# A hybrid decoder layer on one core: moving operands stored as two runs, even and odd columns, and another table of loading rates

## The chip, the core and the metric

The kernel runs on one core of a Trainium2 chip. The core has a matrix engine (TensorE: PE in the profile for its products, PEld for the loads of its stationary operand), a vector engine (VectorE, DVE), a scalar engine (ScalarE, ACT), GpSimd (POOL) and a sync engine (SyncE, SP), which here issues the transfers. Sixteen DMA engines move data between main memory and the on-chip memory; products are summed in an accumulation memory of eight banks. The metric is the device time of one launch in microseconds (us), the median of several runs; lower is better.

## The reference

One decoder layer over 256 tokens of width 2048, in float32. A condition vector `c` yields nine modulation vectors, three for each of three blocks:

```python
cond = jax.nn.silu(c)
mod = cond @ ada_w[l] + ada_b[l]
sh1, sc1, gt1, sh2, sc2, gt2, sh3, sc3, gt3 = jnp.split(mod, N_MOD, axis=-1)
h = ada_in(x, norm_g[l, 0], sh1, sc1)              # rmsnorm(x) * g * (1 + sc) + sh
x = x + MACARON_W * gt1[:, None, :] * swiglu(h, ffn_w_gate[l, 0], ffn_w_up[l, 0], ffn_w_down[l, 0])
h = ada_in(x, norm_g[l, 1], sh2, sc2)
x = x + gt2[:, None, :] * hybrid_mixer(h, ...)     # 8 heads of attention with forgetting, 8 of a gated delta rule
h = ada_in(x, norm_g[l, 2], sh3, sc3)
x = x + MACARON_W * gt3[:, None, :] * swiglu(h, ffn_w_gate[l, 1], ffn_w_up[l, 1], ffn_w_down[l, 1])
return rmsnorm(x, final_norm)
```

`swiglu(h)` is `(silu(h @ wg) * (h @ wu)) @ wd` with an inner width of 5632. The three matrices of each SwiGLU, the mixer's input projection and its output projection are nearly all of the arithmetic; `ada_w` (2048 by 18432) is a matrix that meets a single vector.

## The kernel before, in words

**Layout.** Activations stand with features on the 128 partitions and tokens in the columns: `x` is 16 feature blocks (`k`) of 256 tokens. A weight matrix is cut into tiles of 128 by 128, 5392 in all. The host packs them in the order of use, eight to a block, so that 674 blocks of 512 KB are read one after the other.

**Products in two parts.** Each operand is split into a high part, which is its rounding to `fp32r`, the form in which TensorE takes a float32 operand in one pass, and a low part, which is what the rounding left. A product is high x high + high x low + low x high. `hs` holds the modulated input, per `k` 256 columns of the low part (`LO`) and then 256 of the high part (`HI`), with 64 columns of room behind them; `hid` holds the inner activations of a SwiGLU and `oh` the outputs of the heads, as [high | low], 256 columns each. The weight tile is the stationary operand and the activation is the moving one, column by column as it lies in memory, except in `project_rows` (the mixer's z and v parts), where a slice of 128 tokens of `hs` is stationary and 512 columns of weights move.

The shapes of the products are three. `gate_up_first` (the gate and up products of the first part of SwiGLU_1, lines 518 to 520) and `project` (the mixer's input projection, lines 706 to 708) give a weight tile three products of 256 columns. `mm_h` (the other gate and up products, lines 432 and 433) and `mm` (the down products and the output projection, lines 436 and 437) give it one of 512 columns, both parts of the activation side by side, and one of 256. `Early.products` (the first group of SwiGLU_2, lines 376 to 378) has three products, two of them of 258 columns, since two columns with the shift vector ride along.

**The stream of weights.** `Stream.block` issues the transfer of a block (`wraw`, line 96) and has ACT make its high part (`whi`, line 98); `Stream.next` has DVE make its low part (`wlo`, line 110) when the first tile of the block is used. There are four sets of buffers during a SwiGLU and three in the mixer.

**Modulation columns.** `ada_col` loads 128 rows of `ada_w` (1024 KB, into `adat`, line 228) and lets DVE multiply and sum them against `silu(c)` in one instruction (line 230), which gives one column of `mod`. There are 144 such columns. When each is loaded is set by `RATE`: a pair (b, r) says that from weight block b on, r columns are begun per block. `ada_need` brings forward those that a consumer asks for. Weight blocks 0 to 111 are the gate and up products of the first part of SwiGLU_1 (28 of its 44 inner blocks), 112 to 167 the down products of that part, 168 to 263 its second part, 264 on the mixer. Since each load is issued behind the last weight transfer (`issue_after(W.last)`), both kinds share one queue, SP's, in this order.

**Who writes the moving operands.** `modulate_one` (lines 317 to 328) and `Early.y` (lines 351 to 361) write `hs`: ACT the high part, DVE the low part. `split` (lines 449 to 451) writes `hid`, and `out_split` (lines 1070 to 1074) writes `oh`, with one instruction of ACT and one of DVE each.

## Time and profile before

| | us |
|---|---|
| median of 3 runs | 2041.44 |
| lowest and highest | 2040.09, 2043.89 |
| profiled execution, span from first to last instruction | 2038.5 |
| PE busy in it | 1998.6 (98%) |
| PEld busy | 1818.5 (89%) |
| DVE busy | 1566.0 (77%) |
| ACT busy | 1021.5 (50%) |
| POOL busy | 64.7 (3%) |

The profile gives no time of its own for the profiled execution beside its span. The transfers moved 519.56 MB, 255 GB/s on average. A line of the groups reads: line, engine, operation, out<-in, shape, count, then busy time and the mean of one in ns, then the idle time of the engine just before. A matrix product's own duration is longer than the distance to the next one, since products overlap in the array; what a product costs is the distance between starts, which the timeline shows. A window's row gives the busy time of each engine in a stretch of the span with the number of its instructions, then the granted clock as a share of full speed, the share of the DMA engines and what they moved in GB/s.

### The profile page before, as it was taken

To read this page: it belongs to the slowest core of one execution; us is meant where nothing else is said; L and a number is where in the kernel's file an instruction comes from. 1 tells how busy PE (TensorE), PEld (TensorE's weight loads), DVE (VectorE), ACT (ScalarE), POOL (GpSimd) and SP (SyncE) were. 2 spreads that over 40 slices of the span, in tenths; PEclk is the share of its full clock that TensorE was granted. 3 is DMA by queue.
4 is the path that set the end of the run, shared out by engine and by line. 5 is a ranking of instruction groups with operands and counts; after the bars stand their busy time and mean duration, and the time that the engine had idled before them with its cause. 6 is when DMAs were issued, how large, how long until landed. Compare 5 with 4: busy or idle time off the path is not lost.

```text
span 2038.5 us, 33631 instructions
## 1 busy us (share of the span) xinstructions
PE 1998.6 (98%) x13058; PEld 1818.5 (89%) x13059; DVE 1566.0 (77%) x2424; ACT 1021.5 (50%) x1607; POOL 64.7 (3%) x60
## 2 busy tenths in 40 slices
PE   8999999999999999999999999999999999999997
PEld 6999999888888888889989988988888888888886
DVE  6898978889888998779878889976666555555555
ACT  6544544333444446666655655654444344444442
POOL 0000000000000120000000002000000000000012
PEclk9999999999999999999999999999999999999998
DMA  9999867999889885676666668667776655555553
GB/s 338 350 327 327 288 212 262 372 344 368 334 338 331 336 306 187 232 243 236 219 242 221 222 229 304 234 223 241 252 231 218 193 188 189 193 187 191 192 187 113
DMA packets 129489, 519.56 MB, mean 255 GB/s; under 512 B 18217, under 2 KB 21545, under 8 KB 111153
## 3 DMA queue, kind: packets, MB, share of 16 engines
q1 hardware_dynamic: 129330, 517.42, 72.1%
q8 instruction: 102, 1.67, 0.3%
q14 instruction: 57, 0.47, 0.1%
HBM read 512.89 MB, written 4.47 MB: 254 GB/s over the span
## 4 chain that ended last, share of the span: by engine, by line
PE 86%; DVE 6%; ACT 2%; DMA 2%; issue 2%; SPq 0%; DVEq 0%; ACTq 0%
PE pd L436 15%; PE pu L432 10%; PE pg L432 10%; PE pd L437 8%; PE pu L433 5%; PE pg L433 5%; PE pgu L520 5%; PE pgu L518 5%; PE pgu L519 5%; PE pp L706 3%; PE pp L708 3%; PE pp L707 3%; DVE wlo L110 2%; DMA wraw<-in_w_dram 2%; PE po L436 2%
## 5 line engine op out<-in xcount | busy, mean ns | idle before, releaser
L110 DVE TENSOR_TENSOR wlo<-wraw,whi 128x1024 fp32r<-128x1024 f32 x674 | 822.5, 1228 | 307.2 <-ACT whi L98 304.3
L98 ACT CAST whi<-wraw 128x1024 fp32r<-128x1024 f32 x674 | 702.0, 1049 | 630.2 <-issue 153.4
L436 PE MATMUL pd<-hid,whi 128*128 128x512 f32 x1408 | 488.5, 390 | 0.0
L437 PE MATMUL pd<-hid,wlo 128*128 128x256 f32 x1408 | 397.3, 282 | 1.0 <-DVE wlo L110 0.8
L230 DVE CUSTOM_DVE_ANT_0 adat<-adat,cs,colt 128x2048 f32<-128x2048 f32 x140 | 329.3, 2352 | 35.9 <-DMA adat<-in_ada_dram 35.7
L432 PE MATMUL pg<-hs,whi 128*128 128x512 f32 x912 | 318.9, 390 | 0.5 <-DVE shc L384 0.4
L432 PE MATMUL pu<-hs,whi 128*128 128x512 f32 x912 | 318.7, 390 | 0.0
L436 PEld LDWEIGHTS pd<-hid,whi 128*128 128x128 f32 x1408 | 264.1, 188 | 55.0
L437 PEld LDWEIGHTS pd<-hid,wlo 128*128 128x128 f32 x1408 | 266.1, 189 | 3.0 <-DVE wlo L110 2.7
L433 PE MATMUL pg<-hs,wlo 128*128 128x256 f32 x912 | 257.2, 282 | 0.0
L433 PE MATMUL pu<-hs,wlo 128*128 128x256 f32 x912 | 257.1, 282 | 0.0
L518 PE MATMUL pgu<-hs,whi 128*128 128x256 f32 x896 | 249.0, 281 | 6.8 <-ACT hs L323 5.7
L520 PE MATMUL pgu<-hs,wlo 128*128 128x256 f32 x896 | 248.0, 281 | 1.9 <-DVE wlo L110 1.8
L519 PE MATMUL pgu<-hs,whi 128*128 128x256 f32 x896 | 249.8, 281 | 0.0
L432 PEld LDWEIGHTS pg<-hs,whi 128*128 128x128 f32 x912 | 171.1, 188 | 36.7 <-ACT shc L383 0.5
L432 PEld LDWEIGHTS pu<-hs,whi 128*128 128x128 f32 x912 | 171.1, 188 | 35.7
L706 PE MATMUL pp<-hs,whi 128*128 128x256 f32 x656 | 189.7, 290 | 2.4 <-ACT whi L98 1.2
L708 PE MATMUL pp<-hs,wlo 128*128 128x256 f32 x656 | 186.2, 285 | 0.3 <-DVE wlo L110 0.3
L707 PE MATMUL pp<-hs,whi 128*128 128x256 f32 x656 | 185.7, 283 | 0.0
L518 PEld LDWEIGHTS pgu<-hs,whi 128*128 128x128 f32 x896 | 168.7, 189 | 7.7 <-ACT hs L323 6.1
L433 PEld LDWEIGHTS pu<-hs,wlo 128*128 128x128 f32 x912 | 172.3, 189 | 0.2
L433 PEld LDWEIGHTS pg<-hs,wlo 128*128 128x128 f32 x912 | 172.4, 189 | 0.0
(334 smaller groups left out, 2572.0 us busy)
## 6 DMA issues: line engine op xcount, KB each, us to landing
wraw<-in_w_dram SPq DMA_DIRECT2D x674, 512.0 KB, 4.4
adat<-in_ada_dram SPq DMA_DIRECT2D x140, 1024.0 KB, 7.1
xr<-in_xr_dram SPq DMA_DIRECT2D x4, 512.0 KB, 6.3
adaf<-in_ada_dram SPq DMA_DIRECT2D x4, 512.0 KB, 8.7
adaf<-in_ada_dram SPq DMA_DIRECT2D x2, 1024.0 KB, 12.5
xd<-x SPq DMA_DIRECT2D x4, 512.0 KB, 8.3
rw<-rowd SPq DMA_DIRECT2D x16, 128.0 KB, 6.7
x<-xd SPq DMA_DIRECT2D x4, 512.0 KB, 8.8
```

Source lines behind the costliest of these rows:

```text
L98: self.cast = self.nc.scalar.copy(self.h, r).ins
L110: nc.vector.tensor_tensor(self.l, r, self.h.bitcast(F32), ALU.subtract)
L230: V.tensor_tensor_reduce(t, t, cs, 1.0, L("adab", q, 1), ALU.mult, ALU.add, mod[:, q : q + 1])
L432: PE.matmul(ps, wt[0], hs[:, k, ALL], start=(k == 0), stop=False)
L433: PE.matmul(ps[:, T:], wt[1], hs[:, k, HI], start=False, stop=(k == KD - 1))
L436: PE.matmul(ps, wt[0], act.rearrange("p a t -> p (a t)"), start=first, stop=False)
L437: PE.matmul(ps[:, :T], wt[1], act[:, 0], start=False, stop=last)
L518: PE.matmul(o, wh, hs[:, k, HI], start=first and s == 0, stop=False, skip_group_check=skip)
L519: PE.matmul(o, wh, hs[:, k, LO], start=False, stop=False, skip_group_check=skip)
L520: PE.matmul(o, wl, hs[:, k, HI], start=False, stop=last, skip_group_check=skip)
L706: PE.matmul(pp[i][:, :T], wh, hs[:, k, HI], start=(k == 0), stop=False)
L708: PE.matmul(pp[i][:, :T], wl, hs[:, k, HI], start=False, stop=(k == KD - 1))
```

## The change

**The layout.** `hs` now holds, per `k`, four runs of 144 columns: low part even tokens, low part odd tokens, high part even, high part odd; 128 are used (129 in the high part, for the two shift columns). The room per `k` is 576 columns as before. A product reads the two runs of a part in turn, one column from the even run, one from the odd, so that it gets the tokens in the same order as before and its output lies as before. `hid` and `oh` keep their 256 columns a part and hold even tokens in the first 128 and odd ones in the last 128. The writers (`modulate_one`, `Early.y`, `split`, `out_split`) read their sources in order and write into the two runs in turn (`pairs` for the source, `woven` or `part` for the destination). In the mixer's input `hs` stays as it was (`plain`, `weave=False`), since `project_rows` uses it as the stationary operand; there the weights move, and the host packs each 512 of their columns as 256 even ones and 256 odd ones, which are read in turn as well. The three products of `project` read and multiply as before.

No instruction is added or taken away by this, and no size of one changes.

**The rates.** From block 68 to 111 the columns are loaded at 0.2 a block instead of 0.06, from 112 to 167 at 0.38 instead of 0.5, from 168 to 263 at 0.34 instead of 0.38, from 280 to 407 at 0.27 instead of 0.25.

On SP's queue, from the weight blocks of the sixties on (`wraw` are weight blocks, `adat` modulation columns, `cstt` a table of constants of the mixer), before:

```order
L228 DMA adat<-in_ada_dram 128x2048
L96 DMA wraw<-in_w_dram 128x1024 x6
L664 DMA cstt<-in_cst_dram 128x1180
L96 DMA wraw<-in_w_dram 128x1024 x6
L228 DMA adat<-in_ada_dram 128x2048
L96 DMA wraw<-in_w_dram 128x1024 x17
L228 DMA adat<-in_ada_dram 128x2048
L96 DMA wraw<-in_w_dram 128x1024 x16
L228 DMA adat<-in_ada_dram 128x2048
L96 DMA wraw<-in_w_dram 128x1024 x2
```

and after:

```order
L240 DMA adat<-in_ada_dram 128x2048
L107 DMA wraw<-in_w_dram 128x1024 x4
L240 DMA adat<-in_ada_dram 128x2048
L107 DMA wraw<-in_w_dram 128x1024 x4
L683 DMA cstt<-in_cst_dram 128x1180
L107 DMA wraw<-in_w_dram 128x1024
L240 DMA adat<-in_ada_dram 128x2048
L107 DMA wraw<-in_w_dram 128x1024 x5
L240 DMA adat<-in_ada_dram 128x2048
L107 DMA wraw<-in_w_dram 128x1024 x5
```

Where two columns stood between runs of 16 and 17 weight blocks, there is now one for every five; behind block 112, where one stood for every two blocks, there is one for every two or three.

On DVE, at the last sums of the gate and up products of the first part (`tg` and `tu` are the gate and up sums of an inner block, `hid` its activation, `wlo` a weight block's low part, the ISA row with `adat` a modulation column), before:

```order
L536 TENSOR_TENSOR tg_2878<-pgu_2817,acc_425 128x256
L537 TENSOR_TENSOR tu_2879<-pgu_2817,acc_425 128x256
L110 TENSOR_TENSOR wlo_2992<-wraw_2988,whi_2990 128x1024
L467 TENSOR_TENSOR tu_2879<-tu_2879,tg_2878 128x256
L451 TENSOR_TENSOR hid_2884<-tu_2879,hid_2884 128x256
L110 TENSOR_TENSOR wlo_3032<-wraw_3028,whi_3030 128x1024
L230 ISA adat_3064,mod_126<-adat_3064,cs_86,colt_87 128x2048
```

and after:

```order
L121 TENSOR_TENSOR wlo_2965<-wraw_2961,whi_2963 128x1024
L555 TENSOR_TENSOR tg_2881<-pgu_2820,acc_425 128x256
L556 TENSOR_TENSOR tu_2882<-pgu_2820,acc_425 128x256
L242 ISA adat_2967,mod_126<-adat_2967,cs_86,colt_87 128x2048
L242 ISA mod_126 128x1
L486 TENSOR_TENSOR tu_2882<-tu_2882,tg_2881 128x256
L121 TENSOR_TENSOR wlo_2998<-wraw_2994,whi_2996 128x1024
L470 TENSOR_TENSOR hid_2887<-tu_2882,hid_2887 128x128x2
```

A column's product has come in between the sums and the low parts of the weights, and `hid` is written as 128 pairs. On PE the order of the products of the two SwiGLUs stays; in the mixer the heads' small products stand some projection tiles earlier or later in places.

The diff:

```diff
@@ -31,7 +31,7 @@
 GR = 24
 NEG = -1e30
 
-RATE = ((0, 0.5), (24, 0.34), (56, 0.45), (68, 0.06), (112, 0.5), (168, 0.38), (264, 0.1), (280, 0.25), (408, 0.125))
+RATE = ((0, 0.5), (24, 0.34), (56, 0.45), (68, 0.2), (112, 0.38), (168, 0.34), (264, 0.1), (280, 0.27), (408, 0.125))
 N_BIG, N_GDN = 3, 3
 N_FIRST = 4
 AHEAD = 4
@@ -40,7 +40,8 @@
 HIDX = 3
 MORE = True
 
-HS = 2 * 256 + 64
+HA = 128 + 16
+HS = 4 * HA
 PAD = {"hs": 16, "w": 56, "hid": 16, "more": 56}
 
 BACK = (4, 6, 9)
@@ -70,6 +71,16 @@
 N_COL = _n
 
 
+def woven(ap):
+
+    return ap.rearrange("p (a b) -> p b a", a=2)
+
+
+def pairs(ap):
+
+    return ap.rearrange("p (b a) -> p b a", a=2)
+
+
 class Stream:
 
 
@@ -113,9 +124,10 @@
                 self.owed -= 1.0
                 self.side()
         for d in range(width):
-            self.order.append((mat, k, n + d))
+            self.order.append((mat, k, n, width, d))
         o = (i % WB) * P
-        return self.h[:, o : o + width * P], self.l[:, o : o + width * P]
+        h, l = self.h[:, o : o + width * P], self.l[:, o : o + width * P]
+        return (h, l) if width == 1 else (woven(h), woven(l))
 
 
 @with_exitstack
@@ -311,21 +323,27 @@
 
 
     hsf = keep.tile([P, KD * HS + PAD["w"]], F32R, name="hs")
-    hs = hsf[:, : KD * HS].rearrange("p (k i) -> p k i", k=KD)
-    LO, HI, HIS, ALL = slice(0, T), slice(T, 2 * T), slice(T, 2 * T + 2), slice(0, 2 * T)
-
-    def modulate_one(j, g1, sh, r):
+    hs = hsf[:, : KD * HS].rearrange("p (k q a b) -> p k q a b", k=KD, q=2, a=2)
+    LO, HI = 0, 1
+
+    plain = hsf[:, : KD * HS].rearrange("p (k i) -> p k i", k=KD)[:, :, : 2 * T].rearrange("p k (q t) -> p k q t", q=2)
+
+    def part(k, q, extra=0):
+        return hs[:, k, q, :, : P + extra].rearrange("p a b -> p b a")
+
+    def modulate_one(j, g1, sh, r, weave=True):
 
         t = pt("ht")
+        hl, hh, tt = (part(j, LO), part(j, HI), pairs(t)) if weave else (plain[:, j, LO], plain[:, j, HI], t)
         V.scalar_tensor_tensor(t, x[:, j], g1, r, ALU.mult, ALU.mult)
         if j % 2:
             A.activation(t, t, AF.Identity, bias=sh)
-            A.copy(hs[:, j, HI], t)
-            return V.tensor_tensor(hs[:, j, LO], t, hs[:, j, HI].bitcast(F32), ALU.subtract)
+            A.copy(hh, tt)
+            return V.tensor_tensor(hl, tt, hh.bitcast(F32), ALU.subtract)
         else:
             with tc.issue_after(W.cast) if W.first else nullcontext():
-                A.activation(hs[:, j, HI], t, AF.Identity, bias=sh)
-            return V.scalar_tensor_tensor(hs[:, j, LO], t, sh, hs[:, j, HI].bitcast(F32), ALU.add, ALU.subtract)
+                A.activation(hh, tt, AF.Identity, bias=sh)
+            return V.scalar_tensor_tensor(hl, tt, sh, hh.bitcast(F32), ALU.add, ALU.subtract)
 
     def gains(which, m_sc, j, n):
 
...
@@ -354,11 +372,11 @@
             ada_need(self.m_sh, KD - 1)
             if j == 0:
                 sh = mod[:, self.m_sh * KD : (self.m_sh + 1) * KD]
-                A.copy(hs[:, :, 2 * T], sh)
-                V.tensor_sub(hs[:, :, 2 * T + 1], sh, hs[:, :, 2 * T].bitcast(F32))
+                A.copy(hs[:, :, HI, 0, P], sh)
+                V.tensor_sub(hs[:, :, HI, 1, P], sh, hs[:, :, HI, 0, P].bitcast(F32))
             g = gains(self.which, self.m_sc, j, 1)
-            A.activation(hs[:, j, HI], x[:, j], AF.Copy, scale=g)
-            V.scalar_tensor_tensor(hs[:, j, LO], x[:, j], g, hs[:, j, HI].bitcast(F32), ALU.mult, ALU.subtract)
+            A.activation(part(j, HI), pairs(x[:, j]), AF.Copy, scale=g)
+            V.scalar_tensor_tensor(part(j, LO), pairs(x[:, j]), g, part(j, HI).bitcast(F32), ALU.mult, ALU.subtract)
 
         def step(self, k):
 
@@ -373,9 +391,9 @@
                 h_upto(min(k, k - 4 + max(0, k - 10)))
 
         def products(self, ps, wt, k):
-            PE.matmul(ps[:, : T + 2], wt[0], hs[:, k, HIS], start=(k == 0), stop=False)
-            PE.matmul(ps[:, :T], wt[0], hs[:, k, LO], start=False, stop=False)
-            PE.matmul(ps[:, : T + 2], wt[1], hs[:, k, HIS], start=False, stop=(k == KD - 1))
+            PE.matmul(ps[:, : T + 2], wt[0], part(k, HI, 1), start=(k == 0), stop=False)
+            PE.matmul(ps[:, :T], wt[0], part(k, LO), start=False, stop=False)
+            PE.matmul(ps[:, : T + 2], wt[1], part(k, HI, 1), start=False, stop=(k == KD - 1))
 
         def scaled(self, dst, ps):
 
@@ -429,12 +447,13 @@
         chains[kind].append((h, chain))
 
     def mm_h(ps, wt, k):
-        PE.matmul(ps, wt[0], hs[:, k, ALL], start=(k == 0), stop=False)
-        PE.matmul(ps[:, T:], wt[1], hs[:, k, HI], start=False, stop=(k == KD - 1))
+        both = hs[:, k, :, :, :P].rearrange("p q a b -> p q b a")
+        PE.matmul(ps, wt[0], both, start=(k == 0), stop=False)
+        PE.matmul(ps[:, T:], wt[1], part(k, HI), start=False, stop=(k == KD - 1))
 
     def mm(ps, wt, act, first, last):
-        PE.matmul(ps, wt[0], act.rearrange("p a t -> p (a t)"), start=first, stop=False)
-        PE.matmul(ps[:, :T], wt[1], act[:, 0], start=False, stop=last)
+        PE.matmul(ps, wt[0], act.rearrange("p q (a b) -> p q b a", a=2), start=first, stop=False)
+        PE.matmul(ps[:, :T], wt[1], woven(act[:, 0]), start=False, stop=last)
 
     def merge(dst, ps, scale=None):
 
@@ -447,8 +466,8 @@
             V.scalar_tensor_tensor(dst, ps[:, :T], scale, t, ALU.mult, ALU.add)
 
     def split(dst, src):
-        A.copy(dst[:, 0], src)
-        V.tensor_sub(dst[:, 1], src, dst[:, 0].bitcast(F32))
+        A.copy(woven(dst[:, 0]), pairs(src))
+        V.tensor_sub(woven(dst[:, 1]), pairs(src), woven(dst[:, 0]).bitcast(F32))
 
     def residual(ps, j, m_gt, half):
         ada_need(m_gt, j)
@@ -515,9 +534,9 @@
             wh, wl = W.next(("gu"[s], 0), k, f)
             first, last = k == k0, k == k1 - 1
             skip = s == 1
-            PE.matmul(o, wh, hs[:, k, HI], start=first and s == 0, stop=False, skip_group_check=skip)
-            PE.matmul(o, wh, hs[:, k, LO], start=False, stop=False, skip_group_check=skip)
-            PE.matmul(o, wl, hs[:, k, HI], start=False, stop=last, skip_group_check=skip)
+            PE.matmul(o, wh, part(k, HI), start=first and s == 0, stop=False, skip_group_check=skip)
+            PE.matmul(o, wh, part(k, LO), start=False, stop=False, skip_group_check=skip)
+            PE.matmul(o, wl, part(k, HI), start=False, stop=last, skip_group_check=skip)
 
         turn = [0]
 
...
@@ -715,10 +734,10 @@
             for k in range(KD):
                 wh, wl = W.next(mat, k, 4 * grp, 4)
                 for t in range(2):
-                    sl = slice(t * P, (t + 1) * P)
-                    PE.matmul(pv[t], hs[:, k, HI][:, sl], wh, start=(k == 0), stop=False)
-                    PE.matmul(pv[t], hs[:, k, HI][:, sl], wl, start=False, stop=False)
-                    PE.matmul(pv[t], hs[:, k, LO][:, sl], wh, start=False, stop=(k == KD - 1))
+                    hh, hl = (plain[:, k, q, t * P : (t + 1) * P] for q in (HI, LO))
+                    PE.matmul(pv[t], hh, wh, start=(k == 0), stop=False)
+                    PE.matmul(pv[t], hh, wl, start=False, stop=False)
+                    PE.matmul(pv[t], hl, wh, start=False, stop=(k == KD - 1))
                     tick(2 * TILE_US)
             return pv
 
@@ -1070,8 +1089,8 @@
         def out_split(i, ps, g):
 
             o = oh_[i] = otile("oh")
-            A.activation(o[:, 0], ps, AF.Copy, scale=g)
-            V.scalar_tensor_tensor(o[:, 1], ps, g, o[:, 0].bitcast(F32), ALU.mult, ALU.subtract)
+            A.activation(woven(o[:, 0]), pairs(ps), AF.Copy, scale=g)
+            V.scalar_tensor_tensor(woven(o[:, 1]), pairs(ps), g, woven(o[:, 0]).bitcast(F32), ALU.mult, ALU.subtract)
 
 
         def fox(h, qk, vt):
@@ -1296,8 +1315,11 @@
         mats[("u", s)] = v["ffn_w_up"][0, s]
         mats[("d", s)] = v["ffn_w_down"][0, s]
     w = np.empty((N_TILES // WB, P, WB, P), np.float32)
-    for i, (m, k, n) in enumerate(order):
-        w[i // WB, :, i % WB] = mats[m][k * P : (k + 1) * P, n * P : (n + 1) * P]
+    for i, (m, k, n, width, d) in enumerate(order):
+        cols = n * P + np.arange(width * P)
+        if width > 1:
+            cols = cols.reshape(-1, 2).T.ravel()
+        w[i // WB, :, i % WB] = mats[m][k * P : (k + 1) * P, cols[d * P : (d + 1) * P]]
     return w.reshape(N_TILES // WB, P, WB * P)
```

8 lines of the change are left out of this document (4 added, 4 removed).

## The prediction

> **What bounds the kernel now.** I read the page's busy times and the chain first, then the products by shape, then the timeline for the distance between their starts, then the windows by stage.
>
> ```profile
> PE 1998.6 (98%) x13058; PEld 1818.5 (89%) x13059; DVE 1566.0 (77%) x2424; ACT 1021.5 (50%) x1607; POOL 64.7 (3%) x60
> ...
> PE 86%; DVE 6%; ACT 2%; DMA 2%; issue 2%; SPq 0%; DVEq 0%; ACTq 0%
> ```
>
> PE makes up 86% of the chain that ended last. So the time is the number of products times the distance between their starts, plus some waits. The products that the change touches are these (TensorE's groups by shape; the stationary operand stands behind the moving one's name):
>
> ```profile
> L436 PE MATMUL pd<-hid,whi 128*128 128x512 f32 x1408 | 488.5, 390 | 0.0
> ...
> L432 PE MATMUL pg<-hs,whi 128*128 128x512 f32 x912 | 318.9, 390 | 0.5 <-DVE shc L384 0.4
> L432 PE MATMUL pu<-hs,whi 128*128 128x512 f32 x912 | 318.7, 390 | 0.0
> ...
> L518 PE MATMUL pgu<-hs,whi 128*128 128x256 f32 x896 | 249.0, 281 | 6.8 <-ACT hs L323 5.7 <-ACT hs L327 1.1
> ...
> L706 PE MATMUL pp<-hs,whi 128*128 128x256 f32 x656 | 189.7, 290 | 2.4 <-ACT whi L98 1.2 <-ACT hs L327 1.1
> ...
> L436 PE MATMUL po<-oh,whi 128*128 128x512 f32 x256 | 89.8, 392 | 0.0
> ...
> L719 PE MATMUL pv<-whi,hs 128*128 128x512 f32 x128 | 52.5, 412 | 2.6 <-DVE cv L857 1.6 <-ACT whi L98 0.9
> ```
>
> By counts: 1408 + 912 + 912 + 256 = 3488 tiles with a product of 512 and one of 256 columns; 896 with three of 256 (SwiGLU_1's first part); 656 of the projection, which the change leaves alone; 128 × 3 = 384 products of 512 columns with weights moving. By the code, `Early.products` adds 96 tiles. PE hardly waits within any group. The durations overlap, so what each costs is read from starts in the timeline:
>
> ```profile
> 300.21 0.28 PE L520 MATMUL pgu<-hs,wlo 128*128 128x256 f32 x1
> ...
> 305.81 0.28 PE L520 MATMUL pgu<-hs,wlo 128*128 128x256 f32 x1
> ```
>
> ```profile
> 1699.73 0.28 PE L433 MATMUL pu<-hs,wlo 128*128 128x256 f32 x1
> ...
> 1707.01 0.28 PE L433 MATMUL pu<-hs,wlo 128*128 128x256 f32 x1
> ```
>
> ```profile
> 20.03 1.46 PE L173 MATMUL zp<-zw 128*128 128x512 bf16 x6
> ...
> L173 PE MATMUL zp<-zw 128*128 128x512 bf16 x6 | 1.5, 379 | 0.1
> ```
>
> Between the first two lie 16 tiles: 5.60 / 16 = 350.0 ns for 3 × 256 columns. Between the next two lie 21 tiles: 7.28 / 21 = 346.7 ns for 512 + 256. Both are 768 columns, so a product costs 3.3 ns of its own and (350.0 − 10) / 768 = 0.443 ns a column. The warm-up products in bf16, two bytes a column, run at (1.46 − 0.379) / 5 = 216.2 ns for 512 columns, (216.2 − 3.3) / 512 = 0.416 ns a column. So a moving column of four bytes costs 6% more than one of two: about one lost column time in 16 columns, or every 64 bytes. It is the same in every tile, whatever DVE, ACT and the transfers do beside it. That makes it look like the reading of the moving operand itself, and that reading is what the change alters.
>
> **The change part by part.**
>
> *Reading two runs in turn.* No instruction is added, removed or resized. Nothing in the profile reads a moving operand in this manner, so its price is bounded from both sides. From below: the bf16 rate, 0.416, where no time is lost. From above, the slowest rate of a product at full clock, plain float32, whose products the trace shows as two records each:
>
> ```profile
> 902.01 0.61 PE L873 MATMUL pkk<-kk 128*128 128x128 f32 x4
> ...
> L873 PE MATMUL pkk<-kk 128*128 128x128 f32 x32 | 5.1, 277 | 0.0
> ...
> 900.83 0.39 PE L719 MATMUL pv<-whi,hs 128*128 128x512 f32 x1
> ...
> 901.76 0.42 PE L720 MATMUL pv<-wlo,hs 128*128 128x512 f32 x1
> ```
>
> (0.61 − 0.277) / 3 = 111 ns for 128 columns, (111 − 3.3) / 128 = 0.84 ns a column, two column times. I take the lower end. The loss comes with the bytes of one run; with two runs read in turn, each has twice as long until it comes to its next 64 bytes, and I expect the next piece of one to be fetched while the other delivers. This is an inference, not a reading, hence the chances below. Saved then: 768 × (0.443 − 0.416) = 20.7 ns a tile. 3488 tiles give 72.2 us, 896 give 18.5, `Early`'s 96 give 2.0. The 384 products with moving weights stand (901.76 − 900.83) / 4 = 232.5 ns apart; at 216.2 they give 6.3. Sum 99.0 us.
>
> [...]
>
> *What gives some of it back.* A faster PE needs its weights sooner. The windows by stage (weight blocks 0 to 24, to 56, to 68, to 112, to 168, to 232, roughly):
>
> ```profile
> 20.00:90.00 70.00, 64.52 (x518) 63.04 (x518) 59.18 (x65) 42.40 (x63) 0.00 (x0) 0.95 0.93 342
> 90.00:180.00 90.00, 86.76 (x736) 85.95 (x735) 86.20 (x103) 37.96 (x42) 0.00 (x0) 1.00 0.92 332
> 180.00:219.00 39.00, 39.00 (x336) 39.00 (x335) 34.05 (x39) 15.72 (x18) 0.00 (x0) 1.00 0.94 340
> 219.00:339.00 120.00, 120.00 (x1031) 120.00 (x1030) 96.37 (x154) 62.87 (x95) 0.00 (x0) 1.00 0.69 228
> 339.00:496.00 157.00, 156.11 (x921) 138.23 (x921) 139.50 (x160) 59.47 (x60) 0.00 (x0) 1.00 0.95 358
> 496.00:675.00 179.00, 178.90 (x1032) 158.39 (x1031) 156.39 (x180) 83.55 (x123) 0.00 (x0) 1.00 0.90 338
> ...
> L110 DVE TENSOR_TENSOR wlo<-wraw,whi 128x1024 fp32r<-128x1024 f32 x674 | 822.5, 1228 | 307.2 <-ACT whi L98 304.3 <-PE po L437 1.4
> L230 DVE CUSTOM_DVE_ANT_0 adat<-adat,cs,colt 128x2048 f32<-128x2048 f32 x140 | 329.3, 2352 | 35.9 <-DMA adat<-in_ada_dram 35.7
> ```
>
> The transfers ran at 358 GB/s in the down products without holding PE (156.11 of 157 us busy). Up to block 24 they run at 342 while PE is already idle for 5 us of 70: I let those 192 tiles gain nothing (−4.0 us). From 24 to 68 DVE is busy 86.20 of 90 us at first and the transfers stand at 332 to 340; I take half of 352 × 20.7 ns (−3.6). In the mixer the chain twice goes through a weight block's transfer at the projections, so half of the 6.3 (−3.1).
>
> ```profile
> 795.96 5.60 DMA wraw<-in_w_dram
> ...
> 854.30 7.74 DMA wraw<-in_w_dram
> ```
>
> The writers of `hs`, `hid` and `oh` now scatter 256 columns into two runs. DVE's reduction at line 912 writes its results 64 bytes apart and its slowest, 225 columns in, takes 381 ns beside 389 for the product of the same 225 at line 911. I take nothing for it. The upper bound is a slow form of such a write, line 361 at 970 ns against 474; half a microsecond more on each of 88 `hid` writes stays beside PE, since DVE has room in all stages but one:
>
> ```profile
> L911 DVE TENSOR_TENSOR x<-x x30: 146/217/389, 852.6 to 939.6; 64x1 f32<-64x1 f32 x2, 64x4 f32<-64x4 f32 x2, 64x9 f32<-64x9 f32 x2, 64x16 f32<-64x16 f32 x2
> L912 DVE TENSOR_REDUCE x<-x x30: 139/214/381, 852.8 to 940.3; 64x1 f32<-64x1 f32 x2, 64x2 f32<-64x4 f32 x2, 64x3 f32<-64x9 f32 x2, 64x4 f32<-64x16 f32 x2
> L361 DVE SCALAR_TENSOR_TENSOR hs<-x,g,hs x16: 474/958/970, 1220.6 to 1292.1; 128x256 fp32r<-128x256 f32 x16
> ```
>
> *The rates.* Blocks 68 to 112 get 44 × 0.14 = 6 more columns. DVE there is busy 96.37 of 120 us, 2.25 us of a block's 2.80; 0.14 × 2.44 (a column's product and its read-out) makes it 2.59, against 2.63 a block for a faster PE. That is nearly full: behind a column's 2.35 us stand a block's low part and the `hid` of the next down products. I charge 1.5 us, with 0 (it fits) and 3.5 (a few such collisions) as ends. In the down products 0.38 asks for (0.524 + 0.38 × 1.049) MB in 2.61 us = 354 GB/s, what ran there before; with 0.5 it would be 402, more than any window shows. So the rates bring nothing alone (PE lacks 0.9 us in 157, of which I take 0.5) and keep the gain from being lost there.
>
> Sum: −99.0 + 4.0 + 3.6 + 3.1 + 1.5 − 0.5 = −87.3 us. The span 2038.5 becomes 1951.2. The median of the runs is 2.9 above that span: 1954 us.
>
> **The rivals.**
>
> *Half of the loss stays.* If the two runs reach the end of their 64 bytes together and both wait, but once for two, 0.443 becomes 0.429: −49.5, some 4 given back, 1996 us. For it speaks that the runs lie 512 to 1024 bytes apart, whole multiples of 64, and so in step; against it, nothing in a row.
>
> *The change does nothing to the reading.* If the loss belongs to the columns and not to where they lie, only the rates act, with up to 0.9 us to win and up to 3.5 to lose: 2041 us, 2037 to 2045. For it: the loss is the same for `hs`, `hid` and both sizes.
>
> *Slower: each column opens another place.* One mechanism: the reader holds one piece of memory at a time, so taking columns in turn costs a fetch a column. It acts in every touched product. At 0.84 ns a tile costs 768 × (0.84 − 0.443) = 305 ns more: 4480 tiles are 1366 us, the 384 products 512 × 0.84 + 3.3 − 232.5 = 201 ns each, 77 us; 3485 us. It decides as soon as more than one column in 16 loses its time, since that is today's loss. For it: today's reading in a row is nearly free. Against it: line 873's products are slow because each takes two passes, not for a pattern of reading, so the price is only a bound. [...] A smaller loss, by crowding on DVE from block 68 to 112 and by slower writes, ends at 2046 to 2060.
>
> **How the numbers follow.** Loss gone: 0.45 (1942 if nothing is given back, with some room below, 1978 if a fifth of the loss stays or blocks 0 to 112 gain nothing). Half: 0.20. Nothing: 0.10, of which 0.04 faster and 0.06 within 0.2% (4 us, about what a measurement of this kernel can tell from no change). A fetch a column: 0.20. A small loss: 0.05. Faster 0.69, same 0.06, slower 0.25. The predicted time is the first case's, 1954; its own range is 1935 to 1978. The range leaves out the fetch a column alone: 1935 to 2060.
>
> **What would show it.** Right: 16 tiles of lines 518 to 520's successors in 5.27 us instead of 5.60, 21 tiles of the `mm_h` pair in 6.85 instead of 7.28, the projection's unchanged at 350 ns a tile; PE still at 97% or more; 350 to 360 GB/s in the first down products. Half: 5.43 and 7.06. Wrong: the same distances, or longer ones; or the distances shorter and PE idle in front of `wlo` from block 24 to 112, which would put the loss in DVE or the transfers.

## The result, and the profile after

The changed kernel takes 1993.39 us (median of 4 runs, 1990.72 to 1996.71), the kernel before 2042.66 beside it (4 runs, 2040.09 to 2045.78): a ratio of 0.976, interval 0.9742 to 0.9777. The profiled execution has a span of 1988.9 us, against 2038.5: 49.6 us less, where 87.3 were forecast. One of the four executions of e4 below ran at a granted clock of 0.681 and took 2696.11 us; the times given for e4 are those of the other three. The page's busy times and its chain:

```profile
PE 1919.0 (96%) x13059; PEld 1787.9 (90%) x13059; DVE 1579.5 (79%) x2424; ACT 1051.1 (53%) x1607; POOL 56.0 (3%) x60
...
PE 66%; DVE 14%; DMA 10%; issue 6%; ACT 4%; SPq 0%; DVEq 0%; ACTq 0%
```

PE still ends the kernel, but the chain runs through it for 66% of the span instead of 86%; DVE went from 6 to 14%, the transfers from 2 to 10%. So PE became faster and now waits. First the products, in the groups by shape:

```profile
L455 PE MATMUL pd<-hid,whi 128*128 128x512 f32 x1408 | 461.9, 382 | 3.8 <-DVE hid L470 3.8
...
L451 PE MATMUL pg<-hs,whi 128*128 128x512 f32 x912 | 303.7, 384 | 4.2 <-DVE shc L402 3.5 <-DVE hs L342 0.7
...
L537 PE MATMUL pgu<-hs,whi 128*128 128x256 f32 x896 | 247.0, 279 | 8.7 <-ACT hs L341 7.0 <-ACT whi L109 1.7
...
L725 PE MATMUL pp<-hs,whi 128*128 128x256 f32 x656 | 189.7, 290 | 2.7 <-ACT whi L109 1.4 <-ACT hs L345 1.1 <-DVE cv L876 0.2
...
L738 PE MATMUL pv<-whi,hs 128*128 128x512 f32 x128 | 50.0, 393 | 0.9 <-DVE cv L876 0.5 <-ACT whi L109 0.5
```

Counts and shapes are the old ones. The mean of a product of 512 columns fell from 390 to 382 and 384, in the row products from 412 to 393; the projection, which still reads in a row, kept its 290. The distances between starts, in the timeline (start, duration):

```profile
192.87 0.28 PE L539 MATMUL pgu<-hs,wlo 128*128 128x256 f32 x1
...
197.89 0.28 PE L539 MATMUL pgu<-hs,wlo 128*128 128x256 f32 x1
...
1700.12 0.27 PE L452 MATMUL pu<-hs,wlo 128*128 128x256 f32 x1
...
1707.00 0.27 PE L452 MATMUL pu<-hs,wlo 128*128 128x256 f32 x1
```

Between the first two lie 15 tiles: 5.02 / 15 = 334.7 ns, before 350.0. Between the next two lie 21: 6.88 / 21 = 327.6, before 346.7. By the starts in the two traces the row products stand 216 ns apart instead of 232.5, and a tile of `Early`'s three products takes 335 ns instead of 353.5. So there was to be gained 3488 × 19.1 = 66.6 us, 896 × 15.3 = 13.7, 384 × 16.5 = 6.3 and 96 × 18.5 = 1.8: 88.4 us. Of these 39 are missing from the span.

Where they are missing is counted on PE. There are 5264 products with the low part of the weights in each of these kernels (128 of them row products), and the start of the n-th one marks the same point of the work in each. Differences to the kernel before, in us of one profile each (e1 to e4 are the experiments below; "full" is the tiles of the stage by the distances above):

```
stage (products with the low part)        before   full  changed    e1     e2     e3     e4
SwiGLU_1 gate and up, blocks 0-24 (192)     75.9   -2.9    -0.8   -0.5   -0.5   -1.4   -1.5
  blocks 24-68 (352)                       125.0   -5.4    -2.6   +0.6    0.0   -2.2   -3.7
  blocks 68-112 (352)                      123.2   -5.4    +5.2   -2.9   +9.3   +6.1   -3.9
SwiGLU_1 first down products (448)         157.8   -8.6    -8.9   -7.0   -2.5  -10.0   -7.4
SwiGLU_1 second gate and up (512)          177.6   -9.8    -9.9   -8.3   -0.1   -9.0   -8.2
SwiGLU_1 second down products (256)         96.0   -4.9    -2.0   -3.2   +1.1   +1.0   -3.2
mixer, projections and rows (784)          413.3   -6.3    -0.5   +1.0   +0.1   -0.2   -1.4
out product (256)                           94.4   -4.9     0.0   +0.1   +0.1   -2.0   -1.2
SwiGLU_2 first gate and up (704)           247.0  -13.4    -4.6   -5.6   -0.3  -10.9  -11.5
SwiGLU_2 all the rest (1408)               503.8  -26.9   -25.5  -26.7   +0.5  -25.0  -26.6
```

Half of the work gains all it can: the whole of SwiGLU_1's first down and second gate products, and SwiGLU_2 behind its beginning. Blocks 68 to 112 lose 5.2 us where 5.4 were to be won; the mixer and the out product gain next to nothing; the first gate products of SwiGLU_2 gain a third. A stage of one profile is good for a few us only: the four runs of the changed kernel themselves lie 6 us apart, and y2 below, which is the same kernel up to weight block 250, has +9.6 in blocks 68 to 112 and +4.0 in the second down products where the table has +5.2 and −2.0. The kernel before varies less: up to there y1 repeats its stages within 0.1 us.

The windows by stage (about blocks 68 to 112, then the first down products; after the engines' busy times stand PE's clock, the transfers' share and GB/s), then the longest waits of PE in the whole span, then those between 220 and 347 us, then DVE's group of column products:

```profile
220.00:347.00 127.00, 119.43 (x1046) 118.47 (x1045) 111.21 (x170) 67.13 (x96) 0.00 (x0) 0.99 0.71 260
347.00:495.00 148.00, 146.89 (x902) 134.43 (x901) 129.53 (x152) 60.92 (x62) 0.00 (x0) 1.00 0.93 350
```

```profile
PE pgu L539 <- DVE wlo L121: 9.1, 9, 2.5
PE pgu L537 <- ACT hs L341: 7.0, 2, 4.4
PE po L456 <- DVE wlo L121: 4.9, 5, 1.9
...
PE pd L455 <- DVE hid L470: 3.8, 2, 2.6
```

```profile
PE pgu L539 <- DVE wlo L121: 5.9, 4, 2.5
PE pgu L537 <- ACT whi L109: 1.7, 1, 1.7
```

```profile
L242 DVE CUSTOM_DVE_ANT_0 adat<-adat,cs,colt 128x2048 f32<-128x2048 f32 x140 | 329.6, 2354 | 67.1 <-DMA adat<-in_ada_dram 66.6
```

From block 68 to 112 PE was busy all of 120 us before; now it lacks 7.6 of 127, DVE is busy 111 of them, and the low parts of the weights are what PE waits for. DVE waits 66.6 us in the whole span for column transfers that have not landed, before 35.7. How the two hang together stands in the chain of work between 219 and 350 us, of which the columns' transfers make up 28.5%. Its last pieces before 345 us (start, length):

```profile
334.32 7.09 DMA adat<-in_ada_dram
341.68 2.04 issue
343.80 1.15 DVE wlo L121
344.99 0.38 PE pgu L539
```

A column lands, DVE multiplies it (the piece called issue), only then makes the low part of a weight block, and PE starts when that is done. Three of PE's four waits for low parts in this window, 3.4 of the 5.9 us, come right behind a column for which DVE itself had waited 0.9 to 2.0 us; the longest, 2.5 us at 237 us, does not.

### The profile page after: what moved, and what is told of

Read it like the earlier page. It is cut to its first block, busy times and chain, and to the rows that moved or that the text cites. A ratio compares the mean times of both kernels' runs of the same rounds, so it can differ in the third digit from the quotient of the medians.

```text
span 1988.9 us, 33660 instructions
## 1 busy us (share of the span) xinstructions
PE 1919.0 (96%) x13059; PEld 1787.9 (90%) x13059; DVE 1579.5 (79%) x2424; ACT 1051.1 (53%) x1607; POOL 56.0 (3%) x60
## 4 chain that ended last, share of the span: by engine, by line
PE 66%; DVE 14%; DMA 10%; issue 6%; ACT 4%; SPq 0%; DVEq 0%; ACTq 0%
PE pd L455 12%; PE pg L451 10%; PE pu L451 10%; PE pd L456 6%; DVE wlo L121 6%; DMA adat<-in_ada_dram 5%; PE pg L452 5%; PE pu L452 5%; DMA wraw<-in_w_dram 5%; PE pp L725 2%; PE pp L727 2%; PE pp L726 2%; DVE adat L242 2%; ACT whi L109 1%; PE pgu L539 1%
## 5 line engine op out<-in xcount | busy, mean ns | idle before, releaser
L455 PE MATMUL pd<-hid,whi 128*128 128x512 f32 x1408 | 461.9, 382 | 3.8 <-DVE hid L470 3.8
L456 PE MATMUL pd<-hid,wlo 128*128 128x256 f32 x1408 | 384.2, 273 | 1.1 <-DVE wlo L121 0.9
L242 DVE CUSTOM_DVE_ANT_0 adat<-adat,cs,colt 128x2048 f32<-128x2048 f32 x140 | 329.6, 2354 | 67.1 <-DMA adat<-in_ada_dram 66.6
L451 PE MATMUL pg<-hs,whi 128*128 128x512 f32 x912 | 303.7, 384 | 4.2 <-DVE shc L402 3.5
L451 PE MATMUL pu<-hs,whi 128*128 128x512 f32 x912 | 301.9, 382 | 0.0
L456 PEld LDWEIGHTS pd<-hid,wlo 128*128 128x128 f32 x1408 | 270.3, 192 | 2.3 <-DVE wlo L121 2.3
L452 PE MATMUL pg<-hs,wlo 128*128 128x256 f32 x912 | 249.4, 273 | 0.0
L452 PE MATMUL pu<-hs,wlo 128*128 128x256 f32 x912 | 248.7, 273 | 0.0
L539 PEld LDWEIGHTS pgu<-hs,wlo 128*128 128x128 f32 x896 | 172.2, 194 | 11.3 <-DVE wlo L121 11.2
L537 PEld LDWEIGHTS pgu<-hs,whi 128*128 128x128 f32 x896 | 173.4, 194 | 9.7 <-ACT hs L341 7.4
```

Of the source, the lines that this page charges most:

```text
L242: V.tensor_tensor_reduce(t, t, cs, 1.0, L("adab", q, 1), ALU.mult, ALU.add, mod[:, q : q + 1])
L451: PE.matmul(ps, wt[0], both, start=(k == 0), stop=False)
L452: PE.matmul(ps[:, T:], wt[1], part(k, HI), start=False, stop=(k == KD - 1))
L455: PE.matmul(ps, wt[0], act.rearrange("p q (a b) -> p q b a", a=2), start=first, stop=False)
L456: PE.matmul(ps[:, :T], wt[1], woven(act[:, 0]), start=False, stop=last)
L537: PE.matmul(o, wh, part(k, HI), start=first and s == 0, stop=False, skip_group_check=skip)
```

## The experiments

Where a ratio has an interval, the run was timed against the kernel before in several rounds; m1, m2, x1, x2, y1 and y2 were run once each.

**m1: the reading and the writing by themselves.** 48 products for each way to read the moving operand, then 12 writes of 128 × 256 by ACT and DVE for each way to fill it:

```diff
+PE.matmul(ps[:, :256], st, mv[:, :256], ...)                                               # L35
+PE.matmul(ps[:, :256], st, runs(128), ...)                 # two runs in turn; 144, 136 below, L39-L47
+PE.matmul(ps[:, :256], st, mv[:, :256].rearrange("p (b a) -> p a b", a=2), ...)            # L51
+PE.matmul(ps[:, :256], st, mv[:, :256].rearrange("p (a b) -> p b a", a=4), ...)            # L55
+PE.matmul(ps[:, :256], st, mv[:, :256].rearrange("p (a b c) -> p b a c", a=2, c=2), ...)   # L59
+PE.matmul(ps[:, :256], sb, mb[:, :256], ...)                                               # L75, bf16
+PE.matmul(ps[:, :256], st, mv[:, :1024].rearrange("p (b a) -> p a b", a=4)[:, 0], ...)     # L79
+A.copy(w0, pairs); V.tensor_sub(w1, pairs, w0.bitcast(F32))      # "turn": into two runs in turn
+A.copy(r0, by_run); V.tensor_sub(r1, by_run, r0.bitcast(F32))    # "byrun": run by run from every second column
```

> The decoder layer is left out; the kernel only times products and writes by themselves: 48 products a pattern with one stationary tile, then 12 writes a form on ACT and on DVE. Theory A (reading one run of four-byte columns loses a column time every 64 bytes, and a second run read in turn hides it): 256 columns in a row about 117 ns apart, two runs in turn 109 to 112 at any distance of the runs (512, 544, 576 bytes), four runs in turn the same, 512 columns 228 to 230 against 216 to 219, bf16 109. Theory B (the distance of the runs decides): 512 and 576 bytes differ from 544 by several ns. [...] Writes: in turn on ACT and DVE 0.2 us longer than in a row (661 against 403 and 620 against 421 in the changed kernel); written run by run from a source read at every second column: the same as in a row if only scattered writing costs, 0.2 longer if scattered reading costs too.

The products of each line and the writes (duration: least, middle, most in ns; start of the first and of the last of 48):

```profile
L35 PE MATMUL psa<-mv,st x48: 278/283/579, 7.7 to 15.1; 128*128 128x256 f32 x48
L39 PE MATMUL psb<-mv,st x48: 275/275/275, 15.3 to 20.5; 128*128 128x256 f32 x48
L51 PE MATMUL pse<-mv,st x48: 405/409/426, 31.3 to 42.2; 128*128 128x256 f32 x48
L55 PE MATMUL psf<-mv,st x48: 307/311/321, 42.4 to 49.2; 128*128 128x256 f32 x48
L59 PE MATMUL psg<-mv,st x48: 334/346/346, 49.3 to 57.1; 128*128 128x256 f32 x48
L75 PE MATMUL psk<-mb,sb x48: 272/273/283, 84.7 to 89.8; 128*128 128x256 bf16 x48
L79 PE MATMUL psl<-mv,st x48: 430/431/472, 89.9 to 100.9; 128*128 128x256 f32 x48
```

```profile
L100 ACT CAST plain<-raw x12: 395/401/454, 8.3 to 23.0; 128x256 fp32r<-128x256 f32 x12
L101 DVE TENSOR_TENSOR plain<-raw,plain x12: 402/410/426, 8.7 to 23.8; 128x256 fp32r<-128x256 f32 x12
L105 ACT CAST turn<-raw x12: 655/665/672, 8.6 to 23.6; 128x256 fp32r<-128x256 f32 x12
L106 DVE TENSOR_TENSOR turn<-raw,turn x12: 624/632/649, 9.3 to 24.3; 128x256 fp32r<-128x256 f32 x12
L110 ACT CAST byrun<-raw x12: 413/423/489, 9.1 to 24.1; 128x256 fp32r<-128x256 f32 x12
L111 DVE TENSOR_TENSOR byrun<-raw,byrun x12: 406/416/427, 9.8 to 24.8; 128x256 fp32r<-128x256 f32 x12
```

(20.5 − 15.3) / 47 is 111 ns for two runs in turn, 111.7 by the single starts, at distances of 512, 544 and 576 bytes alike; in a row it is 117 to 120 once the first products, of up to 579 ns, are over, and 228.2 against 215.8 for 512 columns. bf16 takes 109.4. The two lines for 512 columns, in a row and from two runs:

```profile
L67 PE MATMUL psi<-mv,st x48: 387/389/402, 63.4 to 74.1; 128*128 128x512 f32 x48
L71 PE MATMUL psj<-mv,st x48: 378/379/379, 74.3 to 84.5; 128*128 128x512 f32 x48
```

So two runs do take away the loss, all of it at 512 columns (bf16 216.2 in the kernel before) and all but 2.3 ns at 256. But theory A, by which any second place to read from helps, fails on the other patterns: four runs in turn take 143.5, where it asked for 109 to 112, and pairs of columns from two runs in turn 166.5. Nor does its one lost column time every 64 bytes make up the 10.9 / 47 = 232 of one run whose columns are read 8 bytes apart, or the 11.0 / 47 = 234 of one read 16 bytes apart: from bf16's 109.4 it would give 109.4 × 9 / 8 = 123 and 109.4 × 5 / 4 = 137, an estimate. And the writers pay: in turn 665 and 632 against 401 and 410, while the same layout filled run by run, with every second column read, costs next to nothing (423 and 416).

**e1: the new reading with the old rates.**

```diff
-RATE = (..., (68, 0.2), (112, 0.38), (168, 0.34), (264, 0.1), (280, 0.27), (408, 0.125))
+RATE = (..., (68, 0.06), (112, 0.5), (168, 0.38), (264, 0.1), (280, 0.25), (408, 0.125))
```

> The changed kernel with the table of rates of before. If the rates took the missing 40 us (six columns more between blocks 68 and 112, on a DVE that is nearly full), this is faster than the changed kernel: about 1975 us, with blocks 68 to 112 at 2.70 us a block instead of 2.88. If the rates protect the down products, as the prediction had it, blocks 112 to 168 lose here (0.5 a block asks for 402 GB/s) and it ends at 1995 to 2005.

**e2: the old reading with the new rates.** The kernel before with the new table alone; against the changed kernel all other edits are undone, of which two are shown:

```diff
-PE.matmul(ps, wt[0], act.rearrange("p q (a b) -> p q b a", a=2), start=first, stop=False)
+PE.matmul(ps, wt[0], act.rearrange("p a t -> p (a t)"), start=first, stop=False)
...
-A.copy(woven(dst[:, 0]), pairs(src))
+A.copy(dst[:, 0], src)
```

> The kernel of before with the new table of rates. Prediction: no gain alone, 2037 to 2045 us. If the new rates themselves cost something between blocks 68 and 112: 2045 to 2055. If the evener loading is a gain of its own: under 2035.

e1 took 1985.76 us, ratio 0.9724 (0.971 to 0.9739); e2 2049.16, ratio 1.0038 (1.0019 to 1.0056). So the new rates cost in both layouts, 7.6 us between the medians of e1 and the changed kernel and 6.5 alone. e1 lies between its two expected values: the rates took a part of the missing time, not all of it. In the table the loss sits in one place, blocks 68 to 112: −2.9 against +5.2 in the new layout, 0 against +9.3 in the old. With the new rates ten columns of e2 fall between those blocks instead of four, so 9.3 us are 1.5 us for each of the six more. The first down products, from which the columns were taken, give back 2.5 in the old layout and 1.9 in the new one (−8.9 against −7.0), far less. With the old rate the first down products of e1 ran so:

```profile
341.00:492.00 151.00, 148.79 (x910) 135.34 (x909) 142.26 (x165) 59.88 (x60) 0.00 (x0) 1.00 0.98 379
```

379 GB/s, with PE busy for all but 2.2 of 151 us. And of the old layout with the new rates, what PE waits for between 221 and 351 us:

```profile
PE pgu L520 <- DVE wlo L110: 5.0, 4, 2.2
```

No such wait stood there before. So more columns make the low parts late without the new layout, too.

**e3: the same layout, written run by run.** The writers read every second column and fill each run whole; reading and rates as in the changed kernel:

```diff
 def pairs(ap):
-    return ap.rearrange("p (b a) -> p b a", a=2)
+    return ap.rearrange("p (b a) -> p a b", a=2)
+def halves_of(ap):
+    return ap.rearrange("p (a b) -> p a b", a=2)
...
-        A.copy(woven(dst[:, 0]), pairs(src))
-        V.tensor_sub(woven(dst[:, 1]), pairs(src), woven(dst[:, 0]).bitcast(F32))
+        A.copy(halves_of(dst[:, 0]), pairs(src))
+        V.tensor_sub(halves_of(dst[:, 1]), pairs(src), halves_of(dst[:, 0]).bitcast(F32))
```

> The changed kernel with the same layout, but its writers fill the even run whole and then the odd run, reading their source at every second column, where the changed kernel writes into both runs in turn. If the scattered writing (0.2 us more on each of ACT and DVE) delays PE: 1975 to 1988 us, with the hid writes back at 420 and 400 ns. If the writes stay beside other work: within 4 us of the changed kernel. If reading every second column costs as much as writing did: the same times and the same 0.2 us.

The `hid` writers in the groups by shape, of the kernel before, of the changed one and of e3:

```profile
L451 DVE TENSOR_TENSOR hid<-tu,hid 128x256 fp32r<-128x256 f32 x88 | 36.9, 421 | 10.4 <-ACT hid L450 10.4
L450 ACT CAST hid<-tu 128x256 fp32r<-128x256 f32 x88 | 35.4, 403 | 68.3 <-DVE tu L467 66.4 <-DVE tu L493 1.9
```

```profile
L469 ACT CAST hid<-tu 128x256 fp32r<-128x256 f32 x88 | 57.7, 661 | 56.1 <-DVE tu L486 54.6 <-DVE tu L512 1.3
L470 DVE TENSOR_TENSOR hid<-tu,hid 128x256 fp32r<-128x256 f32 x88 | 54.2, 620 | 7.0 <-ACT hid L469 6.8
```

```profile
L475 ACT CAST hid<-tu 128x256 fp32r<-128x256 f32 x88 | 38.0, 434 | 67.2 <-DVE tu L492 65.9 <-DVE tu L518 1.3
L476 DVE TENSOR_TENSOR hid<-tu,hid 128x256 fp32r<-128x256 f32 x88 | 37.0, 422 | 4.6 <-ACT hid L475 4.5
```

Here the scattered write cost 199 ns on DVE and 258 on ACT, 88 times each, and e3 has it back. The time was 1989.48 us, ratio 0.9748 (0.9732 to 0.9765), which can't be told from the changed kernel's; the 1975 to 1988 us expected if the writes delay PE were missed. One stage differs: SwiGLU_2's first gate products gain 10.9 instead of 4.6 us, because in the first 176 of these tiles the changed kernel takes 69.5 us and e3 63.3 (before 64.0). The other profiles fall in line: e1, which writes in turn, 67.5; e4 and e5, which write run by run, 62.5 and 64.7.

**e4: both, writers run by run and the old rates.** The edits of e1 and e3 together.

> The changed layout, written run by run, with the table of rates of before. If the two gains add (the old rates gave 7.6 us against the changed kernel, the writers 4): 1978 to 1984 us. If both are the same microseconds of DVE between blocks 68 and 112: 1984 to 1988.

1971.62 us (1970.28 to 1978.33), ratio 0.9673 (0.9642 to 0.9703). This is faster than both kernels, and its interval lies wholly below that of e1, which differs from it in the writers alone: 0.0051 of 2042 us, about 10 us. It also lies below the 1978 to 1984 expected of a plain sum: by the ratios, against the changed kernel, the old rates alone bring 7 us, the other writers alone 2 to 3, and both 18. So the slower writers cost more under the old rates than under the new ones; why is not shown. Of the 88.4 us that the products offer, 70.0 are in e4's span; where the other 18 go was not tried. Its chain:

```profile
PE 74%; DVE 11%; DMA 7%; issue 4%; ACT 3%; SPq 0%; DVEq 0%; ACTq 0%
```

**e5: rates in between.** As e4, with `(68, 0.06), (112, 0.44), (168, 0.4)`.

> As the last one, with 0.06 from block 68, 0.44 from 112, 0.4 from 168 and 0.25 from 280. If the first down products, once PE is faster, are held by the transfers at 0.5 a block (with the old rates they took 2.73 to 2.79 us a block, with 0.38 2.43 to 2.68): 3 to 6 us under the one with the old rates. If the columns cost the same wherever they lie: within 3 us of it.

1976.95 us, ratio 0.9703 (0.9669 to 0.9738): not to be told from e4. The first down products themselves took 147.9 us instead of 150.4, but the total does not show it: between 0.44 and 0.5 columns a block there nothing is to be won that this could measure. What does matter, by e1 and e2, is to keep the columns out of blocks 68 to 112.

**x1 and x2: are the columns too many bytes, or too much work for DVE?** x1 transfers half of each column and lets DVE multiply as long as before; x2 transfers all and multiplies half.

```diff
 x1:
-            t = adap.tile([P, D], F32, name="adat")
+            t = adap.tile([P, D // 2], F32, name="adat")
...
+                    nc.sync.dma_start(t, adaw[i][:, : D // 2])
+                tv, src, cv_ = junk_ada, t.unsqueeze(1).to_broadcast([P, 2, D // 2]), cs.rearrange(...)
 x2:
-            V.tensor_tensor_reduce(t, t, cs, 1.0, L("adab", q, 1), ALU.mult, ALU.add, mod[:, q : q + 1])
+            n = D if i < 4 else D // 2
+            V.tensor_tensor_reduce(t[:, :n], t[:, :n], cs[:, :n], 1.0, ...)
```

> The changed kernel, but of each modulation column's 1024 KB only the first half is loaded, and DVE multiplies that half twice, so its work stays; the modulation values are not the reference's. Theory D (the stages up to block 124 gain nothing since DVE waits there for a column's transfer, with the weights' low parts queued behind it): DVE's wait for adat falls from 67 us to under 20 and blocks 24 to 124 take at least 12 us less than in the changed kernel. Theory V (DVE's own work fills those stages): blocks 24 to 124 stay within 4 us.

> The changed kernel with whole transfers, but DVE multiplies and sums only half of each modulation column (about 1.25 us instead of 2.35); the modulation values are not the reference's. Theory V: blocks 24 to 124 take at least 12 us less than in the changed kernel. Theory D: within 4 us, with DVE's wait for adat as long as before or longer.

x1 took 2022.82 us, x2 1976.98. From x1, the waits of DVE and the transfers' issues:

```profile
DVE junk_ada L243 <- DMA adat<-in_ada_dram: 103.5, 67, 3.3
```

```profile
adat<-in_ada_dram SPq DMA_DIRECT2D x140, 512.0 KB, 5.1
```

Neither theory has what it asked for: blocks 24 to 124 took 283.0 us in the changed kernel, 290.5 in x1 and 276.2 in x2, some 7.5 more and 6.8 less, where each theory asked for 12 less in one of them and no more than 4 of change in the other. In x1 a column lands 5.1 us after its issue instead of 7.4, and still DVE waits longer for columns, 103.5 us. So fewer bytes do not end the wait. That the kernel became slower by 29 us I can't put down to one thing: among 1166 instructions of DVE compared (columns, low parts, the work on `hid`), some 200 come in another order in x1 than in the changed kernel, and as many in x2; e1 has exactly the order of the kernel before, e2 and e3 that of the changed one, and those compare cleanly. In x2 gate and up of SwiGLU_1 took 317.6 us against 325.9, most of it before block 68; in blocks 68 to 112 it gained 2.9 of the 8.1 that the old rates gain. DVE's work is likely a part of it, but with another order and one run this is not shown. That a column whose transfer has not landed holds up the low part behind it in DVE's queue is seen in the changed kernel's chain above (the transfer that lasts 7.09 us from 334.32 us on, the low part at 343.80); what makes the transfers late is open.

**m2: two readers?** The slow patterns of m1 led to another theory. Like m1, the first kernel of this kind, m2 leaves the decoder out; it issues 48 products of 256 columns of four bytes for each of ten ways to read the moving operand, after 64 products in bf16:

```diff
+a flat(256)                                                      # L47, a row
+c flat(128).unsqueeze(2).to_broadcast([P, 128, 2])               # L57, each column twice
+d flat(512).rearrange("p (a b c) -> p b a c", a=2, c=2)[..., 0]  # L62, two runs, every 2nd column
+e flat(1024).rearrange("p (a b c) -> p b a c", a=2, c=4)[..., 0] # L67, two runs, every 4th column
+g flat(512).rearrange("p (b a) -> p b a", a=2)[:, :, 0]          # L77, one run, every 2nd column
+h flat(256).rearrange("p (a b) -> p b a", a=8)                   # L82, eight runs
+j two runs 132 columns apart                                     # L92
```

> [...] Theory R (two readers, one for the columns that come first, third and so on and one for the second, fourth and so on; each is fast as long as at least two of its columns in a row come from the same 16 bytes): a row 117 ns between starts, two runs in turn 111.7, each of 128 columns twice in turn 111.7, two runs of which every second column is read 117 as in a row (each reader takes 8 bytes a step), two runs of which every fourth column is read 230 (16 bytes a step), a row written as pairs 117, every second column of one run 230, runs 129 or 132 columns apart 111.7, eight runs of 32 no better than the four runs' 143.5. [...] Theory A of before (two runs hide the loss at any distance of the columns within a run): all cases with two runs 111.7, the one with every fourth column too. What tells R from A is every second and every fourth column of two runs: 117 and 230 by R, 111.7 twice by A. Twelve writes that fill each run whole from every second column: 436 ns on ACT and 416 on DVE, as in the first kernel.

```profile
L47 PE MATMUL psa<-mv,st x48: 278/283/469, 24.5 to 30.3; 128*128 128x256 f32 x48
L57 PE MATMUL psc<-mv,st x48: 275/275/276, 35.5 to 40.7; 128*128 128x256 f32 x48
L62 PE MATMUL psd<-mv,st x48: 279/283/284, 40.8 to 46.5; 128*128 128x256 f32 x48
L67 PE MATMUL pse<-mv,st x48: 391/407/410, 46.6 to 57.2; 128*128 128x256 f32 x48
L77 PE MATMUL psg<-mv,st x48: 391/407/410, 63.2 to 73.9; 128*128 128x256 f32 x48
L82 PE MATMUL psh<-mv,st x48: 402/418/419, 74.1 to 84.6; 128*128 128x256 f32 x48
L92 PE MATMUL psj<-mv,st x48: 274/275/276, 90.2 to 95.4; 128*128 128x256 f32 x48
```

A row takes 120 ns in the middle, each column twice 111.7, two runs at every second column 119.8, two runs at every fourth (46.6 to 57.2) / 47 = 226, one run at every second column 226, eight runs 223, runs 129 and 132 columns apart 112. The pair that tells the theories apart came out for two readers: two runs are no help as soon as each is read 8 bytes a column (119.8, like the row's 120), and at 16 bytes a column they are as slow as one run (226 both). In these patterns the times go by the step from a column to the next but one, which is the step of each supposed reader: 112 ns at 4 bytes, 120 at 8, 223 to 226 at 16 and more. The 143.5 ns of m1's four runs in turn, where each reader would change its place at every column, do not fit, nor do the 166.5 of its pairs: by the theory they would be at twice the time, as the eight runs are (223). So what the theory says of readers and of 16 bytes is not shown; shown are the times by the step.

**y1 and y2: is the mixer held by the columns?** The kernel before and the changed kernel, both without the last 52 columns:

```diff
+        if i >= 92:
+            if (m, j) in ada_done:
+                ada_done[m, j]()
+            return
```

> The kernel before, with the last 52 of the 144 modulation columns left out, transfer and product both (they take a constant in place of what they would compute; POOL fills it in at the start). These are the columns that fall into the mixer, the out product and SwiGLU_2. It is the control for the run after it. Theory M (in the mixer the columns on DVE and in the transfers take the room in which weights would be made ready): the mixer's 413 us and the out product's 94 become shorter by themselves, by 10 us or more together, in this kernel already. Theory C (there a chain of dependent work on all engines sets the time, whatever the products cost): less than 4 us. SwiGLU_2 waits for nothing before, so nothing there by either.

> The changed kernel with the same 52 columns left out. What counts is its difference to the run before it in the mixer and the out product, where the changed kernel is 0.5 us faster than the kernel before, though its products there should save 13 (384 row products, 96 early tiles, 256 tiles of the out product). Theory M: with room on DVE the difference becomes 8 to 13 us. Theory C: it stays between 0 and 4. In the first quarter of SwiGLU_2, where the changed kernel loses 5.5 us, theory M lets it gain 3.4; a writer of hs that is slower in itself leaves it behind all the same.

2026.72 and 1979.26 us. By the starts of the products:

```
stage                        before  changed     y1     y2   y2 - y1
mixer, projections and rows   413.3    412.8  402.7  404.0      +1.3
out product                    94.4     94.4   92.6   89.3      -3.3
SwiGLU_2, first 176 tiles      64.0     69.5   63.6   62.1      -1.5
```

Neither theory has it whole. The late columns cost the mixer about 10 us in both layouts, but without them the faster row products still shorten nothing there. What else sets the mixer's time in both kernels was not tried. In the out product 3.3 of 4.9 us appear when the columns are gone; that is no more than single profiles differ there (97.7 us in e5, 93.2 in e4), so it is a hint only. And the first tiles of SwiGLU_2 lose nothing any more, 62.1 us, though the writers are still the slow ones; by this and e3's 63.3 it takes both, slow writers and columns, to hold PE up.

## Why the prediction was right, and where it was wrong

**Direction and place were right, the size was not.** 1993 lies in the range of 1935 to 2060, but that range held large gains, no change and a small loss; it does not lie in the likeliest case's own, 1935 to 1978. It lies next to the rival "half of the loss stays" (1996), and that is chance: that one put 49.5 us into the products and nearly no waiting, and the runs show 88.4 us in the products and 39 of waiting. Its signs were 16 tiles in 5.43 us and 21 in 7.06; PE shows 16 × 334.7 = 5.35 and 6.88. "Loss gone" asked for 5.27 and 6.85, so the 21 tiles speak for it and the 16 lie halfway. The total alone would have confirmed the wrong mechanism. The prediction's own sign of being wrong, shorter distances with PE idle in front of `wlo`, came true from block 68 to 112; PE is busy 96%, not 97.

**Reading two runs in turn: right.** 88.4 us instead of 99.0. What was mis-sized is a product of 256 columns: 334.7 / 3 − 256 × 0.416 = 5.1 ns beside its columns where 3.3 was taken, three times in a tile of the first part and once in every other; a product of 512 is as forecast, 215.8 in m1. The reason given, that one run's next piece is fetched while the other delivers, was an inference, and no run shows it. Two readers would sort the patterns of m1 and m2 better (111.7 to 120 ns, 223 to 234), and even so not all of them (127.0, 143.5 and 166.5).

**"The writers … I take nothing for it": the first step that failed.** Line 912's reduction with 381 ns was taken as the near row, but by the kernel it reads 225 columns and writes only 15, so it says little of a write of 256; a write into two runs in turn costs 620 to 661. The upper bound (half a microsecond more, beside PE) was wide enough for the duration, but not the sentence that it "stays beside PE": with the old rates it takes some 10 us (e4 against e1), with the new ones 6 in one profile's first tiles of SwiGLU_2, which the total of e3 does not show.

**The rates: the second.** 1.5 us with 3.5 as the upper end were charged for blocks 68 to 112; they took 8 to 9 (e1, e2). The reckoning of 2.59 us of DVE's time in a block of 2.63 left 0.04 free; it was called nearly full and still priced at a few collisions. It counted DVE's work alone and not its waits for columns that had not landed, 7.4 us in this stage. And "keep the gain from being lost there", said of the down products, rested on 358 GB/s as the most that the transfers do; e1 ran them at 379 and won 7.0 of 8.6 us there. That window had measured what was asked for, not what was possible.

**What comes late in other stages: the third.** For the mixer 3.1 us were given back and 5.8 are lost, and for the out product (4.9 lost) and the second down products of SwiGLU_1 (2.9) nothing was charged. All of PE's groups there waited little before, and this was read as PE being their limit; y1 shows that the mixer gains 10 us from less of other work with the same products. What holds the faster PE up there stays open. Up to block 68 the 7.6 given back were too many: 4.9 are missing.

**The other rivals.** "The change does nothing to the reading" falls with the distances (334.7 and 327.6 ns a tile instead of 350.0 and 346.7). "Each column opens another place" (3485 us) falls with m1: runs 512 bytes apart read in turn are the fast case, 111.7 ns against 117 to 120 in a row. Its 0.84 ns a column was that of one of the two records of a plain float32 product, whose whole price is thus about 222 ns for 128 columns; only this rival's own time rested on it. That the reader holds one piece of memory at a time was its assumption; no run shows it.

## What to carry to other kernels

When the engine that bounds a kernel becomes faster by a few per cent, add up its gain by stage and set beside each stage how full the next engine is: here a stage with 0.04 us to spare in a block was a full one, the more so as its engine also waited for transfers (7.4 us from block 68 to 112). A layout that suits the reader must be priced at the writer too, and which side takes the stride can be chosen: reading every second column and writing whole runs was nearly free here (416 to 423 ns against 401 to 410 in a row, m1), writing in turn was not (632 to 665). A transfer rate that a window shows can be what was asked for (358 GB/s in the first down products before, 379 there in e1); it may be taken for a limit only where the engine behind it was waiting.

## What the runs showed of the hardware that had not been expected

- 256 moving columns of four bytes took, by the step from a column to the next but one (m1 and m2): 111.7 to 112 ns at 4 bytes (bf16 in a row 109.4), 117 to 120 at 8 bytes, 223 to 234 at 16 bytes and more. Four runs in turn (143.5), pairs from two runs (166.5) and fours from two runs (127.0) are not explained by this: the step alone would put the first two at the double.
- A write of 128 × 256 in four bytes into two runs 512 bytes apart in turn took 632 ns on DVE and 665 on ACT, against 410 and 401 in a row and 416 and 423 run by run from every second column (m1).
- Weights and columns came in at 379 GB/s over 151 us in the first down products (e1), where the same products before had 358 over 157 us.
